# First loads of a decoder layer: x and the first weights in smaller pieces, ahead of the other loads

## The chip, the core and the metric

The program runs on one core of a Trainium2 chip. The metric is the device time of one execution in microseconds (us), lower is better; the median of three executions before the change is 1202.25 us. TensorE (PE) multiplies matrices, VectorE (DVE) and ScalarE (ACT) do elementwise work, GpSimd (POOL) does little here, and SyncE (SP) issues nearly all transfers between HBM and the on-chip memory SBUF. PSUM is the memory that TensorE accumulates in.

## The reference

One layer of a decoder with 16 learned tokens put ahead of 256 input tokens (with 112 inert slots of padding in front, which the kernel leaves out: it works on T = 272 columns). Cut to what matters:

```
u    = rmsnorm(h, attn_norm) * vmask          # h: tokens x 2048
proj = u @ w_in                               # 2048 x 6144
aq, ak, av, rq, rk, rv, rg = split(proj)
ya = rmsnorm(diff_attention(aq, ak, av, lam, slopes, valid), attn_subln) * (1 - lam_init)
yr = rmsnorm(retention(rq, rk, rv, log_g), ret_norm) * silu(rg)
h  = h + concat(ya, yr) @ w_out
u  = rmsnorm(h, ffn_norm) * vmask
h  = h + (silu(conv(u @ w_gate)) * (u @ w_up)) @ w_down
out = rmsnorm(h, final_norm)[:, padding + 16:]
```

Everything is float32. `diff_attention` adds a distance term to the scores (ALiBi), which the kernel reads from a prepared array, `alibi`.

## The kernel before

All products are made in three passes of a rounded format: each operand is split into a high part and a remainder, and hi*hi, hi*lo and lo*hi are summed in PSUM. For a weight chunk (1024 KB, 128 partitions x 2048 columns, tile `raw`) ACT casts a half of 1024 columns into `whi`, and DVE subtracts to give `wlo`; for x, ACT scales a k-tile of 128 features (`xhi`) and DVE makes `xlo`. `raw`, `whi` and `wlo` have three buffers each, so the cast of a half waits until PE is through with the half three before it.

There are 48 chunks of input projection, 16 of `w_out`, 88 of gate and up, 44 of `w_down`. The norm of x is not applied ahead of the first product: the outputs are multiplied by `rstd1` afterwards, and `rstd1` comes from the squares of x, summed by ACT and DVE into `acc`, summed over partitions by a matmul with `ones` (tile `psx`, L204), and put through a chain of twelve DVE operations (from `ms`, L206, to `rstd`, L127).

The change lies in the start, a loop over four blocks `c` of four k-tiles each. Since x arrives together with the weights here, the first four output tiles (`mm_93` to `mm_96`) are accumulated side by side: for each k-tile 12 matmuls (4 tiles x 3 passes, L189 to L191). `w_first[c]` is a 1024 KB chunk that holds the four tiles' weights of block `c`. After the start, `gemm` computes one output tile per chunk (L261 to L263), 48 matmuls each: the fifth tile from the first chunk of `w_in`, and so on; `prep` (L99, L100) splits their weights. In the text, "chunk 4" is the first of `w_in`, "chunk 7" the fourth.

SP issues the transfers in the order in which they stand. A load into `raw` waits until the buffer's former content has been split. The constants `lq`, `c_ident`, `c_alibi`, `c_attn_subln`, `c_ret_norm`, `c_ffn_norm` and `c_conv_w` are loaded on the same queue. `c_alibi` has 86 partitions; all other loads of the start have 128. ACT needs it for `bias` (L302), DVE needs `c_attn_subln` for a small scaling (L233).

A scheduler merges the program's parts into one instruction order for each engine; each engine then runs in that order and waits on semaphores. `klz`, a small tile of the attention, and later `htok`, which holds the residual by tokens, share one room of the pool `big` (tag `htok`).

Of the kernel before, what the change touches and what calls it, by code (L numbers as in the profile page):

```python
# [10 lines left out]
F32 = mybir.dt.float32  # L11
# [3 lines left out]
AF = mybir.ActivationFunctionType  # L15
ALU = mybir.AluOpType
# [3 lines left out]
P = 128  # L20
D = 2048
# [3 lines left out]
T = META + SEQ  # L25
# [28 lines left out]
def trunk_kernel(ctx, tc, a, out):  # L54
    nc = tc.nc
    V, S, PE = nc.vector, nc.scalar, nc.tensor

    cp = ctx.enter_context(tc.tile_pool(name="const", bufs=1))
    big = ctx.enter_context(tc.tile_pool(name="big", bufs=1))
    wp = ctx.enter_context(tc.tile_pool(name="wts", bufs=1))  # L60
# [19 lines left out]
    raw = {}  # L80
# [24 lines left out]
    def ahead(hf):  # L105
        while state["dma"] < len(chunks) and state["dma"] <= (hf + 4) // 2:
            load(state["dma"])
            state["dma"] += 1
        while state["prep"] < 2 * len(chunks) and state["prep"] <= hf + 2:
            prep(state["prep"])  # L110
            state["prep"] += 1

    def rsqrt(x, shape, pool, tag, o=None, tags=None):
        tags = tags or (tag + "i", tag + "t", tag + "o")
        i = pool.tile(shape, I32, tag=tags[0], name=tag + "i")
        V.tensor_scalar(out=i, in0=x.bitcast(I32), scalar1=1, scalar2=None,
                        op0=ALU.logical_shift_right)
        V.tensor_scalar(out=i, in0=i, scalar1=-1, scalar2=0x5F3759DF,
                        op0=ALU.mult, op1=ALU.add)
        y = i.bitcast(F32)  # L120
        t = pool.tile(shape, F32, tag=tags[1], name=tag + "t")
        if o is None:
            o = pool.tile(shape, F32, tag=tags[2], name=tag + "o")
        for it in range(3):
            V.scalar_tensor_tensor(out=t, in0=y, scalar=-0.5, in1=x, op0=ALU.mult, op1=ALU.mult)
            V.tensor_tensor(out=t, in0=t, in1=y, op=ALU.mult)
            V.scalar_tensor_tensor(out=o, in0=t, scalar=1.5, in1=y, op0=ALU.add, op1=ALU.mult)  # L127
            y = o
        return o
# [26 lines left out]
    FN = [(Q0, NQ), (0, T), (0, T), (Q0, NQ)]  # L156
    with tc.tile_pool(name="start", bufs=2) as st:
        acc = st.tile([P, 4, T], F32, name="acc", bufs=1)
        for c in range(4):
            xr = st.tile([P, 4, T + 1], F32, tag="xr", bufs=4, name=f"xr{c}")  # L160
            rw = wp.tile([P, D], F32, tag="raw", bufs=3, name=f"raw{c}")
            cuts = [(0, 1), (1, 2), (2, 4)] if c == 0 else [(0, 2), (2, 4)] if c == 1 else [(0, 4)]
            for b, e in cuts:
                nc.sync.dma_start(out=xr[:, b:e], in_=a["x"][:, 4 * c + b:4 * c + e])
                nc.sync.dma_start(out=rw[:, b * 512:e * 512], in_=a["w_first"][c][:, b * 512:e * 512])  # L165
            for half in range(2):
                whi = wp.tile([P, 1024], F32R, tag="whi", bufs=3, name=f"whi{2 * c + half}")
                wlo = wp.tile([P, 1024], F32R, tag="wlo", bufs=3, name=f"wlo{2 * c + half}")
                for jj in range(2):
                    j = 2 * half + jj  # L170
                    k = 4 * c + j
                    xg = xr[:, j, T:T + 1]
                    S.activation(out=xhi[:, k], in_=xr[:, j, :T], func=AF.Copy, scale=xg)
                    V.scalar_tensor_tensor(out=xlo[:, k], in0=xr[:, j, :T], scalar=xg,
                                           in1=xhi[:, k].bitcast(F32),
                                           op0=ALU.mult, op1=ALU.subtract)
                    if c == 0 or jj == 0:
                        n = 512 if c == 0 else 1024
                        d = slice(jj * 512, jj * 512 + n)
                        src = rw[:, j * 512:j * 512 + n]  # L180
                        S.copy(out=whi[:, d], in_=src)
                        V.tensor_tensor(out=wlo[:, d], in0=src, in1=whi[:, d].bitcast(F32),
                                        op=ALU.subtract)
                    for t, (t0, n) in enumerate(FN):
                        b = jj * 512 + t * P
                        wh, wl = whi[:, b:b + P], wlo[:, b:b + P]
                        xh, xl = xhi[:, k, t0:t0 + n], xlo[:, k, t0:t0 + n]
                        o = first[t][:, :n]
                        PE.matmul(o, wh, xh, start=(k == 0), stop=False)  # L189
                        PE.matmul(o, wh, xl, start=False, stop=False)  # L190
                        PE.matmul(o, wl, xh, start=False, stop=(k == KT - 1))  # L191
            if c == 0:
                S.activation(out=acc, in_=xr[:, :, :T], func=AF.Square)
            else:
                sq = st.tile([P, 4, T], F32, tag="sq", name=f"sq{c}")
                S.activation(out=sq, in_=xr[:, :, :T], func=AF.Square)
                V.tensor_tensor(out=acc, in0=acc, in1=sq, op=ALU.add)
        state["dma"], state["prep"] = 4, 8
        ahead(8)
        with tc.high_priority():  # L200
            V.tensor_tensor(out=acc[:, 0:2], in0=acc[:, 0:2], in1=acc[:, 2:4], op=ALU.add)
            V.tensor_tensor(out=acc[:, 0], in0=acc[:, 0], in1=acc[:, 1], op=ALU.add)
            pst = psx[:, 0]
            PE.matmul(pst[:, :T], ones, acc[:, 0], start=True, stop=True)  # L204
            ms = st.tile([P, T], F32, name="ms", bufs=1)
            V.tensor_scalar(out=ms, in0=pst[:, :T], scalar1=EPS, scalar2=None, op0=ALU.add)  # L206
            rsqrt(ms, [P, T], st, "r1", rstd1)
# [60 lines left out]
    with ExitStack() as p1:  # L268
# [211 lines left out]
        for h in range(AH):  # L480
            q = ap_.tile([P, NQ], F32, tag="q", name=f"q{h}")
            k = ap_.tile([P, T], F32, tag="k", name=f"k{h}")
# [12 lines left out]
            for m in range(2):  # L495
# [3 lines left out]
                                op=ALU.subtract)  # L499
# [3 lines left out]
                                op=ALU.subtract)  # L503
            side.extend(att_tasks(h, q2, (k2, kl), v))
        for kind, r in RSEQ:
# [9 lines left out]
            k = ap_.tile([P, T], F32, tag="k", name=f"rk{r}")  # L515
# [18 lines left out]
        htok = big.tile([P, 2, D], F32, tag="htok", name="htok")  # L534
        acc2 = yp.tile([P, NQ], F32, name="acc2")
        for j in range(KT):
            xr = ap_.tile([P, NQ], F32, tag="g0", name=f"xres{j}")
# [6 lines left out]
            else:  # L544
                sq = ap_.tile([P, NQ], F32, tag="rt", bufs=4, name=f"hsq{j}")
# [4 lines left out]
                                   in1=ghi[:, j].bitcast(F32), op0=ALU.mult, op1=ALU.subtract)  # L550
# [16 lines left out]
    with ExitStack() as p2:  # L567
# [4 lines left out]
        for f in range(NF):  # L572
# [3 lines left out]
            c = fw.tile([P, SEQ], F32, tag="c", name=f"fc{f}")  # L576
            V.tensor_scalar(out=c, in0=g[:, 0:SEQ], scalar1=cw[:, f, 0:1], scalar2=None,
                            op0=ALU.mult)
            for i in (1, 2):
                V.scalar_tensor_tensor(out=c, in0=g[:, i:i + SEQ], scalar=cw[:, f, i:i + 1],  # L580
                                       in1=c, op0=ALU.mult, op1=ALU.add)
# [8 lines left out]
                            op=ALU.subtract)  # L590
# [138 lines left out]
def build(arrs):  # L729
    import concourse.bacc as _bacc  # L730
    import concourse.tile as _tile
    from concourse import mybir as _mybir

    nc = _bacc.Bacc("TRN2", target_bir_lowering=False, num_devices=1)
    arrays, args = {}, {}
    for name, v in arrs.items():
        arrays[f"in_{name}_dram"] = v
        args[name] = nc.dram_tensor(f"in_{name}_dram", v.shape, _mybir.dt.from_np(v.dtype),
                                    kind="ExternalInput").ap()
    o = nc.dram_tensor("out_0_dram", (SEQ, D), _mybir.dt.from_np(np.dtype("float32")),  # L740
                       kind="ExternalOutput").ap()
    with _tile.TileContext(nc, schedule_with_timeline_sim=True) as tc:
        trunk_kernel(tc, args, o)
    return nc, arrays
# [8 lines left out]
```

## Time and profile before

| | us |
|---|---|
| median of 3 runs (1201.59 to 1203.49) | 1202.25 |
| the profiled execution | 1201.67 |
| its span, first to last instruction | 1199.9 |
| PE busy in it | 1183.2 |
| DVE busy | 790.1 |
| ACT busy | 557.5 |

The span is what the rows below divide up; 1.77 us of the profiled execution lie outside of it. All stretches are given in us from the span's start. In the timeline the starts of successive matmuls show their pace better than their lengths, since they overlap.

### The profile page before, as it was taken

How to read it: one execution, taken by the hardware profiler on the slowest of the kernel's cores; microseconds unless marked ns; L12 is line 12 of the kernel's file. 1: busy time of each engine (PE TensorE's matmuls, PEld its weight loads, DVE VectorE, ACT ScalarE, POOL GpSimd, SP SyncE). 2: the span in 40 equal slices, each digit the busy share in tenths (PEclk: the TensorE clock that was granted, in tenths of full speed). 3: DMA queues.
4: the chain of work that ended last, by engine and by line, in shares of the span. 5: the costliest groups of instructions: out<-in, count | busy, mean ns of one | idle time of the engine just before them, and what ended most of it. 6: DMA issues, size and time to landing. Idle time of an engine off the chain costs nothing.

```text
span 1199.9 us, 21288 instructions
## 1 busy us (share of the span) xinstructions
PE 1183.2 (99%) x8811; PEld 1132.3 (94%) x8811; DVE 790.1 (66%) x1423; ACT 557.5 (46%) x865; POOL 2.0 (0%) x7
## 2 busy tenths in 40 slices
PE   8999999999999999999999999999999999999996
PEld 7999999999999999999999999999999988888885
DVE  6888887668766667666666666666666545454544
ACT  6476665554445544444444444444444434343442
POOL 0000000000000000000000000000000000000000
PEclk9999999999999999999999999999999999999999
DMA  8443434444446554555555554555555655555452
GB/s 298 154 169 141 161 131 178 145 156 172 141 159 232 198 187 176 176 188 192 183 176 181 195 188 176 179 196 186 177 181 190 227 177 196 189 179 203 179 189 92
DMA packets 34817, 215.71 MB, mean 180 GB/s; under 512 B 4194, under 2 KB 7882, under 8 KB 9760
## 3 DMA queue, kind: packets, MB, share of 16 engines
q1 hardware_dynamic: 34288, 212.58, 50.2%
q8 instruction: 69, 1.13, 0.4%
q0 software_dynamic: 144, 1.05, 0.2%
q10 hardware_dynamic: 288, 0.72, 0.2%
q14 instruction: 28, 0.23, 0.1%
HBM read 212.24 MB, written 2.10 MB: 179 GB/s over the span
## 4 chain that ended last, share of the span: by engine, by line
PE 95%; DMA 2%; DVE 2%; SPq 0%; ACT 0%; issue 0%; DVEq 0%; ACTq 0%
PE mm L261 24%; PE mm L262 24%; PE mm L263 23%; PE o L612 7%; PE o L614 7%; PE o L613 7%; DMA raw<-in_w_first_dram 1%; PE po L365 1%; DMA xr<-in_x_dram 1%; PE sc L315 0%; PE sc L313 0%; DVE wlo L100 0%; PE pa L353 0%; PE rs L405 0%; SPq L165 0%
## 5 line engine op out<-in xcount | busy, mean ns | idle before, releaser
L99 ACT CAST whi<-raw 128x1024 fp32r<-128x1024 f32 x381 | 399.7, 1049 | 553.4 <-PE mm L262 296.7
L100 DVE TENSOR_TENSOR wlo<-raw,whi 128x1024 fp32r<-128x1024 f32 x381 | 466.2, 1224 | 275.7 <-ACT whi L99 272.4
L261 PE MATMUL mm<-ghi,whi 128*128 128x258 f32 (+1 forms) x1408 | 396.9, 282 | 0.0
L263 PE MATMUL mm<-ghi,wlo 128*128 128x258 f32 (+1 forms) x1408 | 396.7, 282 | 0.0
L262 PE MATMUL mm<-glo,whi 128*128 128x258 f32 (+1 forms) x1408 | 396.1, 281 | 0.0
L262 PEld LDWEIGHTS mm<-glo,whi 128*128 128x128 f32 x1408 | 266.4, 189 | 0.0
L261 PEld LDWEIGHTS mm<-ghi,whi 128*128 128x128 f32 x1408 | 266.0, 189 | 0.0
L263 PEld LDWEIGHTS mm<-ghi,wlo 128*128 128x128 f32 x1408 | 265.8, 189 | 0.0
L261 PE MATMUL mm<-xhi,whi 128*128 128x272 f32 (+1 forms) x688 | 200.4, 291 | 0.0
L262 PE MATMUL mm<-xlo,whi 128*128 128x272 f32 (+1 forms) x688 | 198.8, 289 | 0.0
L263 PE MATMUL mm<-xhi,wlo 128*128 128x272 f32 (+1 forms) x688 | 197.8, 288 | 0.5 <-DVE wlo L100 0.5
L613 PE MATMUL o<-wlo,fhi 128*128 128x512 f32 x340 | 134.2, 395 | 0.0
L614 PE MATMUL o<-whi,flo 128*128 128x512 f32 x340 | 134.1, 395 | 0.0
L263 PEld LDWEIGHTS mm<-xhi,wlo 128*128 128x128 f32 x688 | 129.5, 188 | 0.8 <-DVE wlo L100 0.8
L261 PEld LDWEIGHTS mm<-xhi,whi 128*128 128x128 f32 x688 | 129.7, 188 | 0.1
L262 PEld LDWEIGHTS mm<-xlo,whi 128*128 128x128 f32 x688 | 129.6, 188 | 0.1
L612 PE MATMUL o<-whi,fhi 128*128 128x512 f32 x340 | 120.8, 395 | 0.0
L614 PEld LDWEIGHTS o<-whi,flo 128*128 128x128 f32 x340 | 64.1, 188 | 15.0
L613 PEld LDWEIGHTS o<-wlo,fhi 128*128 128x128 f32 x340 | 64.1, 188 | 14.9
L612 PEld LDWEIGHTS o<-whi,fhi 128*128 128x128 f32 x340 | 64.0, 188 | 14.9
L261 PE MATMUL mm<-yhi,whi 128*128 128x258 f32 x256 | 73.2, 288 | 0.4 <-ACT whi L99 0.4
L262 PE MATMUL mm<-ylo,whi 128*128 128x258 f32 x256 | 72.3, 283 | 0.0
(227 smaller groups left out, 1070.0 us busy)
## 6 DMA issues: line engine op xcount, KB each, us to landing
raw<-in_w_in_dram SPq DMA_DIRECT2D x44, 1024.0 KB, 4.9
raw<-in_w_gate_dram SPq DMA_DIRECT2D x44, 1024.0 KB, 4.9
raw<-in_w_up_dram SPq DMA_DIRECT2D x44, 1024.0 KB, 4.8
raw<-in_w_down_dram SPq DMA_DIRECT2D x44, 1024.0 KB, 4.8
raw<-in_w_out_dram SPq DMA_DIRECT2D x16, 1024.0 KB, 4.8
xres<-in_x_dram SPq DMA_DIRECT2D x16, 129.0 KB, 3.8
raw<-in_w_first_dram SPq DMA_DIRECT2D x2, 1024.0 KB, 13.3
raw<-in_w_first_dram SPq DMA_DIRECT2D x3, 512.0 KB, 7.4
```

The costliest lines, as they stand in the source:

```text
L99: S.copy(out=hi, in_=src)
L100: V.tensor_tensor(out=lo, in0=src, in1=hi.bitcast(F32), op=ALU.subtract)
L261: PE.matmul(ps[:, :n], wh, xh, start=(k == 0), stop=False)
L262: PE.matmul(ps[:, :n], wh, xl, start=False, stop=False)
L263: PE.matmul(ps[:, :n], wl, xh, start=False, stop=(k == KT - 1))
L365: PE.matmul(ps[:QT, i * P:(i + 1) * P], at[j][:n, i - j], vt[:n, j], start=(j == 0), stop=(j == i))
L612: PE.matmul(po[m], ah, wh, start=(k == 0), stop=False)
L613: PE.matmul(po[m], ah, wl, start=False, stop=False)
L614: PE.matmul(po[m], al, wh, start=False, stop=(k == NF - 1))
```

## The change

The transfers of all four blocks are issued ahead of the arithmetic loop, so that they stand in front of all other loads. The first block comes in four pieces of one k-tile, the others in two pieces of two k-tiles. The first piece of x is issued from ACT's queue, and the first piece of weights is cut into two of 256 columns, which ACT and DVE split one by one. The fourth chunk `raw3` gets no buffer of the three in `raw`: it lies in the room of `klz` and `htok`, so it doesn't wait for a buffer. The squares of x stand behind all four blocks in the code.

```
+        xrs, rws = [], []
         for c in range(4):
             xr = st.tile([P, 4, T + 1], F32, tag="xr", bufs=4, name=f"xr{c}")
-            rw = wp.tile([P, D], F32, tag="raw", bufs=3, name=f"raw{c}")
-            cuts = [(0, 1), (1, 2), (2, 4)] if c == 0 else [(0, 2), (2, 4)] if c == 1 else [(0, 4)]
+            if c < 3:
+                rw = wp.tile([P, D], F32, tag="raw", bufs=3, name=f"raw{c}")
+            else:
+                rw = big.tile([P, D], F32, tag="htok", name="raw3")
+            cuts = [(b, b + 1) for b in range(4)] if c == 0 else [(0, 2), (2, 4)]
             for b, e in cuts:
-                nc.sync.dma_start(out=xr[:, b:e], in_=a["x"][:, 4 * c + b:4 * c + e])
-                nc.sync.dma_start(out=rw[:, b * 512:e * 512], in_=a["w_first"][c][:, b * 512:e * 512])
+                lead = c == 0 and b == 0
+                (nc.scalar if lead else nc.sync).dma_start(
+                    out=xr[:, b:e], in_=a["x"][:, 4 * c + b:4 * c + e])
+                step = 256 if lead else (e - b) * 512
+                for d in range(b * 512, e * 512, step):
+                    nc.sync.dma_start(out=rw[:, d:d + step], in_=a["w_first"][c][:, d:d + step])
+            xrs.append(xr)
+            rws.append(rw)
+        for c in range(4):
+            xr, rw = xrs[c], rws[c]
...
                     if c == 0 or jj == 0:
                         n = 512 if c == 0 else 1024
-                        d = slice(jj * 512, jj * 512 + n)
-                        src = rw[:, j * 512:j * 512 + n]
-                        S.copy(out=whi[:, d], in_=src)
-                        V.tensor_tensor(out=wlo[:, d], in0=src, in1=whi[:, d].bitcast(F32),
-                                        op=ALU.subtract)
+                        step = 256 if k == 0 else n
+                        for b in range(0, n, step):
...
+        for c in range(4):
             if c == 0:
-                S.activation(out=acc, in_=xr[:, :, :T], func=AF.Square)
+                S.activation(out=acc, in_=xrs[c][:, :, :T], func=AF.Square)
```

**SP's queue.** Before, from the third block on (`raw_252` is its weights, `raw_323` those of the fourth block, `raw_393` is chunk 4):

```order
L165 DMA raw_252<-in_w_first_dram 128x2048
L164 DMA xr_322<-in_x_dram 128x1092
L215 DMA lq<-in_lambda_qk_dram 128x256
L211 DMA c_ident<-in_ident_dram 128x128
L211 DMA c_alibi<-in_alibi_dram 86x816
L211 DMA c_attn_subln<-in_attn_subln_dram 128x1
L211 DMA c_ret_norm<-in_ret_norm_dram 128x2
L165 DMA raw_323<-in_w_first_dram 128x2048
L211 DMA c_ffn_norm<-in_ffn_norm_dram 128x16
L211 DMA c_conv_w<-in_conv_w_dram 128x132
L87 DMA raw_393<-in_w_in_dram 128x2048
```

And now, from the last half of the fourth block (`raw_125`; `raw_402` is chunk 4, `raw_404` chunk 5):

```order
L169 DMA xr_124<-in_x_dram 128x546
L173 DMA raw_125<-in_w_first_dram 128x1024
L87 DMA raw_402<-in_w_in_dram 128x2048
L230 DMA lq<-in_lambda_qk_dram 128x256
L226 DMA c_ident<-in_ident_dram 128x128
L226 DMA c_alibi<-in_alibi_dram 86x816
L226 DMA c_attn_subln<-in_attn_subln_dram 128x1
L226 DMA c_ret_norm<-in_ret_norm_dram 128x2
L226 DMA c_ffn_norm<-in_ffn_norm_dram 128x16
L226 DMA c_conv_w<-in_conv_w_dram 128x132
L87 DMA raw_404<-in_w_in_dram 128x2048
```

The fourth block and chunk 4 have moved ahead of the constants; the chunk behind them is now chunk 5.

**ACT, end of the start.** Before (`whi_326`, `whi_358`: fourth block; `whi_399`, `whi_403`: chunk 4):

```order
L196 ACTIVATE sq_390<-xr_322 128x1088
L302 ACTIVATE bias_479<-c_alibi 86x816
L230 ACTIVATE lam<-lam 128x2
L181 CAST whi_326<-raw_323 128x1024
L181 CAST whi_358<-raw_323 128x1024
L99 CAST whi_399<-raw_393 128x1024
L99 CAST whi_403<-raw_393 128x1024
```

Now (`whi_328`, `whi_360`: fourth block; `whi_408`, `whi_412`: chunk 4; `whi_416`: chunk 5):

```order
L195 CAST whi_328<-raw_125 128x1024
L185 ACTIVATE xhi_68<-xr_124 128x272 x2
L211 ACTIVATE sq_399<-xr_124 128x1088
L195 CAST whi_360<-raw_125 128x1024
L99 CAST whi_408<-raw_402 128x1024
L317 ACTIVATE bias_488<-c_alibi 86x816
L99 CAST whi_412<-raw_402 128x1024
L245 ACTIVATE lam<-lam 128x2
L99 CAST whi_416<-raw_404 128x1024
```

The operation that needs `c_alibi` has moved behind the fourth block's casts, between the two casts of chunk 4.

**DVE, from chunk 5 to chunk 7.** Before, the first half of chunk 7 (`wlo_701`) stands behind the attention's operands of two heads:

```order
L501 CAST k_0_464<-k_458 64x272 x2
L100 TENSOR_TENSOR wlo_640<-raw_397,whi_639 128x1024
L498 TENSOR_TENSOR q_0_463<-q_457,q_0_463 64x258 x2
...
L344 COPY vt_475<-pv_603 100x128
L345 COPY vt_475<-pv_603 86x256
L100 TENSOR_TENSOR wlo_701<-raw_585,whi_700 128x1024
L100 TENSOR_TENSOR wlo_736<-raw_585,whi_735 128x1024
```

Now the first half of chunk 7 is `wlo_710`, the second `wlo_745`:

```order
L516 CAST k_0_473<-k_467 64x272 x2
L100 TENSOR_TENSOR wlo_710<-raw_594,whi_709 128x1024
L513 TENSOR_TENSOR q_0_472<-q_466,q_0_472 64x258
...
L359 COPY vt_484<-pv_612 100x128
L360 COPY vt_484<-pv_612 86x256
L100 TENSOR_TENSOR wlo_745<-raw_594,whi_744 128x1024
```

The first half of chunk 7 has moved ahead of those operands, and only the second half stands behind them. Further up, `wlo_417` (first half of chunk 5) now stands ahead of `ms`, where `wlo_404` (second half of chunk 4) stood; the matmul on `psx` has moved on PE from inside the fourth block to the thirteenth matmul of the fifth tile that stands behind that block.

## Rows read from the trace of the kernel before

**Rows 1.** The page: busy us, share of the span, instructions.

```profile
PE 1183.2 (99%) x8811; PEld 1132.3 (94%) x8811; DVE 790.1 (66%) x1423; ACT 557.5 (46%) x865; POOL 2.0 (0%) x7
```

**Rows 2.** PE's waits in the whole span: us in total, times, longest.

```profile
PE mm L189 <- ACT whi L181: 3.7, 2, 3.2
...
PE mm L191 <- DVE wlo L182: 0.7, 1, 0.7
PE mm L263 <- DVE wlo L100: 0.5, 1, 0.5
```

**Rows 3.** Timeline of PE: start, us, instruction, [idle before, releaser].

```profile
17.61 0.66 PE L191 MATMUL mm<-xhi,wlo 128*128 128x258 f32 x4
...
22.05 0.28 PE L189 MATMUL mm<-xhi,whi 128*128 128x258 f32 x1
...
23.52 0.28 PE L189 MATMUL mm<-xhi,whi 128*128 128x258 f32 x1
...
29.77 0.39 PE L189 MATMUL mm<-xhi,whi 128*128 128x258 f32 x1 [3.16 <-ACT whi L181]
...
36.96 0.62 PE L204 MATMUL psx<-acc,ones 128*128 128x272 f32 x2
...
37.54 0.29 PE L190 MATMUL mm<-xlo,whi 128*128 128x272 f32 x1
...
38.16 0.29 PE L263 MATMUL mm<-xhi,wlo 128*128 128x272 f32 x1
...
56.21 0.29 PE L262 MATMUL mm<-xlo,whi 128*128 128x272 f32 x1
57.03 0.39 PE L263 MATMUL mm<-xhi,wlo 128*128 128x272 f32 x1 [0.54 <-DVE wlo L100]
```

**Rows 4.** Stretches: busy time of each engine, granted clock, DMA share, GB/s.

```profile
5.00:10.60 5.60, 5.41 (x24) 5.26 (x24) 2.88 (x7) 3.77 (x8) 0.00 (x0) 1.00 0.92 301
11.00:15.00 4.00, 4.00 (x34) 4.00 (x34) 3.68 (x8) 3.98 (x8) 0.00 (x0) 1.00 1.03 424
15.00:18.00 3.00, 3.00 (x27) 3.00 (x26) 3.00 (x5) 3.00 (x6) 0.00 (x0) 1.00 1.01 406
...
30.80:34.10 3.30, 3.30 (x16) 3.08 (x16) 3.30 (x5) 1.05 (x1) 0.00 (x0) 0.50 0.17 50
```

**Rows 5.** Timeline of ACT: the second block's last cast, then the waits.

```profile
14.74 1.04 ACT L181 CAST whi<-raw 128x1024 fp32r<-128x1024 f32 x1
...
26.04 0.89 ACT L302 ACTIVATE bias<-c_alibi 86x816 f32<-86x816 f32 x1 [3.04 <-DMA c_alibi<-in_alibi_dram]
...
28.67 2.00 ACT L181 CAST whi<-raw 128x1024 fp32r<-128x1024 f32 x2 [1.66 <-DMA raw<-in_w_first_dram]
```

**Rows 6.** Timeline of SP's queue: start and us of an issue.

```profile
10.04 0.33 SPq L211 DMA_DIRECT2D c_ident<-in_ident_dram  x1
15.28 0.33 SPq L165 DMA_DIRECT2D raw<-in_w_first_dram  x1
```

**Rows 7.** Transfers: KB of one, median us from issue to landing.

```profile
c_alibi<-in_alibi_dram SPq DMA_DIRECT2D x1, 274.1 KB
...
c_ident<-in_ident_dram SPq DMA_DIRECT2D x1, 64.0 KB, 9.5
```

**Rows 8.** Timeline of DVE.

```profile
14.17 0.91 DVE L174 SCALAR_TENSOR_TENSOR xlo<-xr,xhi 128x272 fp32r<-128x272 f32 x2
15.00 1.28 DVE L197 TENSOR_TENSOR acc<-acc,sq 128x1088 f32<-128x1088 f32 x1
16.20 1.22 DVE L182 TENSOR_TENSOR wlo<-raw,whi 128x1024 fp32r<-128x1024 f32 x1
...
37.62 0.44 DVE L206 TENSOR_SCALAR ms<-psx 128x272 f32<-128x272 f32 x1 [0.73 <-PE psx L204]
...
55.75 2.36 DVE L100 TENSOR_TENSOR wlo<-raw,whi 128x1024 fp32r<-128x1024 f32 x2
```

More of the change, by code (lines that the diff above doesn't have):

```diff
@@ L178, in trunk_kernel @@
                         n = 512 if c == 0 else 1024
-                        d = slice(jj * 512, jj * 512 + n)
-                        src = rw[:, j * 512:j * 512 + n]
-                        S.copy(out=whi[:, d], in_=src)
-                        V.tensor_tensor(out=wlo[:, d], in0=src, in1=whi[:, d].bitcast(F32),
-                                        op=ALU.subtract)
+                        step = 256 if k == 0 else n
+                        for b in range(0, n, step):
+                            d = slice(jj * 512 + b, jj * 512 + b + step)
+                            src = rw[:, j * 512 + b:j * 512 + b + step]
+                            S.copy(out=whi[:, d], in_=src)
+                            V.tensor_tensor(out=wlo[:, d], in0=src, in1=whi[:, d].bitcast(F32),
+                                            op=ALU.subtract)
                     for t, (t0, n) in enumerate(FN):
@@ L191, in trunk_kernel @@
                         PE.matmul(o, wl, xh, start=False, stop=(k == KT - 1))
+        for c in range(4):
             if c == 0:
-                S.activation(out=acc, in_=xr[:, :, :T], func=AF.Square)
+                S.activation(out=acc, in_=xrs[c][:, :, :T], func=AF.Square)
             else:
                 sq = st.tile([P, 4, T], F32, tag="sq", name=f"sq{c}")
-                S.activation(out=sq, in_=xr[:, :, :T], func=AF.Square)
+                S.activation(out=sq, in_=xrs[c][:, :, :T], func=AF.Square)
                 V.tensor_tensor(out=acc, in0=acc, in1=sq, op=ALU.add)
```

## The prediction

> **What bounds the kernel now.** The page comes first: TensorE is busy for 1183.2 of 1199.9 us [rows 1], so a change can win only where it waits or runs slowly. The list of its waits names three that matter: 3.2 us in one piece for a cast of `w_first` weights, 0.7 for a remainder `wlo`, 0.5 for another [rows 2]. The timeline and the stretches place them. The longest ends at 29.77, in front of the fourth block [rows 3]: ACT's cast there waited for the transfer until 28.67 [rows 5]. [...]
>
> Why was the fourth block's chunk late? It was issued at 15.28 [rows 6], behind `c_alibi`, which landed at 26.04; the chunk landed 2.6 us after it [rows 5]. `c_ident`, issued just ahead of `c_alibi`, landed at 10.04 + 9.5 = 19.5 [rows 6, 7]. So 6.5 us passed from the one landing to the next, for 274.1 KB [rows 7]: 43 GB/s, while full stretches move 406 to 424 GB/s [rows 4]. `c_alibi` is a slow transfer, and what is queued behind it waits for a part of it.
>
> [...]
>
> **The start, to 17.6.** I cost the smaller pieces of the first block at nothing, in either direction. What PE does up to 17.61 (four remainders of the second block's second half) is tied to DVE: `xlo` of the block from 14.17, the sum into `acc` from 15.00, `wlo` from 16.20 to 17.42 [rows 8], and PE uses it at 17.61 [rows 3]. On ACT the cast for it follows its neighbours without a gap [rows 5]. The order of these operations is the same after the change, and the bytes of blocks one and two are as many. So an earlier first matmul, or an earlier rise of the clock, ends as a wait in front of this `wlo`. Work that covers it: DVE's chain; without it the gain would be the half microsecond before the first matmul.
>
> **From there to the fifth tile.** Before, PE goes from 17.61 to 38.16, the first matmul with chunk 4's remainder [rows 3], in 20.55 us. Between them lie 114 matmuls of blocks two to four and of the fifth tile, 114 x 0.1225 = 14.0 us, and the `psx` matmul, which moves 0.45 us of time (from 36.96 to the L190 at 37.54, less one matmul of 0.125) [rows 3] behind this point. Can everything now be ready in 14.0 us? Per half-chunk PE needs 24 x 0.1225 = 2.94 us. DVE needs 0.91 for two `xlo`, 1.22 for `wlo`, and half of a sum of 1.28: 2.77 [rows 8]. ACT's cast is 1.04 [rows 5], and its other work is lighter than DVE's. In the new order the operations alternate half by half, so DVE keeps ahead. The fourth block lands about 21.6 (next part) and its second half is wanted at 17.6 + 88 x 0.1225 = 28.4. So the point of 38.16 comes at **31.6**, 6.55 us earlier; `psx` gives 0.45 back, which leaves **6.1**.
>
> **`c_alibi` afterwards.** In front of `c_ident` stand two chunks of 1024 KB more, the fourth block's and chunk 4. 2 x 1.049 MB at 415 GB/s (between 406 and 424 [rows 4]) are 5.05 us, so `c_ident` lands at 24.6 and `c_alibi` at 26.04 + 5.05 = **31.1** (30.9 to 31.5 by the slower and faster rates). Chunk 4 is ahead of it and safe; the fourth block, with one chunk less in front, lands 3 us before `c_ident`. Chunk 5 now stands where the late chunk stood, and lands 2.6 us after `c_alibi`, at 33.7.
>
> Behind ACT's `bias` (0.89 [rows 5]) waits the cast of chunk 4's second half: 31.1 + 0.9 + 1.04 = 33.05, and its `wlo` at 34.3; PE wants the latter at 31.6 + 25 x 0.125 + 0.45 = 35.2. DVE's scaling by `c_attn_subln` lands as late and holds the last sum of `acc` until about 32.0; PE wants it for `psx` at 33.1. Both pass with 0.9 us to spare.
>
> What is late next is the chain of the norm. The cast of chunk 5 ends at 33.7 + 1.05 = 34.75, its `wlo`, which now stands ahead of `ms`, at 36.0, so `ms` starts at 36.0 although `psx` is done by 33.7. Before, DVE went from `ms` at 37.62 to the end of the two `wlo` of chunk 7 at 58.11 [rows 8], 20.5 us; the same list has one `wlo` less now (1.22) and 0.3 us of waits that fall away: 19.0. It ends at 55.0 with the second half of chunk 7. PE reaches that half so: before, it wanted chunk 7's first remainder at 56.21 + 0.125 = 56.33 and got it at 57.03, 0.7 late [rows 3]. From 38.16 to 56.33 are 18.17 us; with `psx` PE is there at 31.6 + 18.17 + 0.45 = 50.2, finds it ready (its place is earlier now), and needs the second half 24 matmuls of 0.125 later, at 53.2. Pause: 55.0 - 53.2 = **1.8 us** in place of 0.7.
>
> **Sum.** 6.1 + 0.7 - 1.8 = **5.0 us**. The rest of the program keeps its order behind the first heads, and PE bounds it. Against the profiled execution's 1201.67 us that gives 1196.6. The median of the runs, 1202.25, is 0.6 above this execution, so I forecast **1197.2 us**.
>
> **Bounds.** Every microsecond by which `c_alibi` lands sooner or later moves the last pause by as much. At 29.3 or sooner there is none: gain 6.8. `klz` is now cleared only after the fourth block is split, on POOL, which has nothing else to do, long before its use; nothing for that. Whether a pause of 1.8 us lowers the clock the trace doesn't show: the 0.7 us one did not (the twelve matmuls from 22.05, right behind it, take 1.47 us [rows 3]), the 3.2 us one did. [...]
>
> **Rivals.**
> [...]
> *No pause at all:* `c_alibi` sooner, or a shorter chain: 1195.4. The margin of 1.8 us is larger than the spread of the transfer rates, which speaks against it.
> *The smaller pieces move slower.* From 5 to 10.6, with the first block's pieces, the stretch has 301 GB/s [rows 4]. If blocks three and four (3.2 MB) moved so, they would take 10.7 instead of 7.8 us, `c_alibi` would land 2.9 us later, and 2.1 us of gain would be left, 1200.1, about no change. Against it: the second block was already cut in two, and the stretch from 11 to 15, where its casts fall, has 424, no less than the 406 after it with whole chunks. [...]
> *Slower than before:* `c_alibi` lands so late that ACT holds chunk 4's second half and PE stands there for over 3 us. [...]
> *The change does nothing:* not possible for the pause before the fourth block, unless the first queue entries wait for landings longer than shown.
>
> **Chances.** Forecast within 1 us of 5.0: 0.5; the clock falls: 0.15; no pause: 0.2; slow pieces: 0.11; slower: 0.04. A measurement of this kernel tells about 0.2% (2.4 us) from no change, so faster is 0.87, the same 0.10, slower 0.03. Eight in ten lie from 1195.0 to 1199.4: the lower end is the gain of 6.8 with 0.4 us for the spread of runs, the upper the fallen clock with `c_alibi` another microsecond late.
>
> **What would show it.** Right: no wait of PE for a cast of `w_first` weights over 0.5 us behind 17.6; no stretch at half clock between 26 and 34; the first matmul with chunk 4's remainder near 31.6; ACT's `bias` idle before it until about 31.1, put down to `c_alibi`; one wait of PE for DVE's `wlo` between 52 and 56, in the second half of chunk 7. Wrong: `bias` starting by 29 or after 33; PE waiting for chunk 4's or 5's cast; a wait in blocks two to four, which would mean that DVE's 2.77 us against 2.94 is too tight.

## The result and the profile after

The changed kernel takes 1196.01 us (median of 4, 1195.63 to 1196.83) where the kernel before took 1202.32 beside it: ratio 0.9948, 95% interval 0.9935 to 0.996. That is 6.3 us faster; 5.0 had been forecast. The profiled execution took 1195.63 us with a span of 1193.9 us.

The page, engines' busy time, to be read against [rows 1]:

```profile
PE 1180.8 (99%) x8811; PEld 1130.6 (95%) x8811; DVE 789.3 (66%) x1424; ACT 557.1 (47%) x866; POOL 2.0 (0%) x7
```

PE's waits (the first is that of the warm-up at the start, as before):

```profile
PE psx L150 <- DVE warm L138: 1.5, 1, 1.5
PE mm L203 <- ACT xhi L185: 0.5, 1, 0.5
PE mm L278 <- DVE wlo L100: 0.4, 1, 0.4
PE mm L276 <- ACT whi L99: 0.4, 1, 0.4
```

The wait of 3.2 us for a cast of `w_first` [rows 2] has gone. The 0.5 is the first matmul of all. The last, for `whi`, was 0.4 us in the kernel before as well. The one for `wlo` is the forecast pause at chunk 7; the timeline of PE has it at the end:

```profile
17.25 0.66 PE L205 MATMUL mm<-xhi,wlo 128*128 128x258 f32 x4
...
31.24 0.29 PE L278 MATMUL mm<-xhi,wlo 128*128 128x272 f32 x1
...
32.75 0.62 PE L219 MATMUL psx<-acc,ones 128*128 128x272 f32 x2
...
53.02 0.29 PE L277 MATMUL mm<-xlo,whi 128*128 128x272 f32 x1
53.76 0.39 PE L278 MATMUL mm<-xhi,wlo 128*128 128x272 f32 x1 [0.45 <-DVE wlo L100]
```

From the second block's remainders to the first remainder of chunk 4 PE needs 31.24 - 17.25 = 13.99 us where it needed 20.55 [rows 3]. The stretches (PE, PEld, DVE, ACT, POOL; then granted clock, DMA share, GB/s) are those of [rows 4] and two more:

```profile
5.00:10.60 5.60, 5.44 (x26) 5.44 (x27) 3.85 (x9) 4.43 (x9) 0.00 (x0) 1.00 0.98 300
11.00:15.00 4.00, 4.00 (x35) 4.00 (x34) 3.71 (x7) 4.00 (x7) 0.00 (x0) 1.00 1.04 416
15.00:18.00 3.00, 3.00 (x27) 3.00 (x26) 3.00 (x5) 3.00 (x7) 0.00 (x0) 1.00 1.03 416
18.00:22.00 4.00, 4.00 (x35) 4.00 (x34) 4.00 (x5) 4.00 (x6) 0.00 (x0) 1.00 1.05 415
24.00:26.00 2.00, 2.00 (x19) 2.00 (x18) 2.00 (x4) 1.32 (x2) 0.00 (x0) 1.00 0.20 73
30.80:34.10 3.30, 3.30 (x27) 3.22 (x27) 1.60 (x3) 2.38 (x4) 0.00 (x0) 1.00 0.54 216
```

The stretch at half clock is gone: 27 matmuls from 30.80 to 34.10 in place of 16. From 24 to 26 the DMA share is only 0.20, at 73 GB/s: what moves there are rows of `c_alibi` and the small constants, and little else was left in the queue. SP issued no load between `c_conv_w` and chunk 5, and the profile puts its wait down to chunk 4's landing (`raw<-in_w_in_dram`):

```profile
21.48 0.33 SPq L226 DMA_DIRECT2D c_conv_w<-in_conv_w_dram  x1
25.15 0.80 SPq L87 DMA_DIRECT2D raw<-in_w_in_dram  x2
```

```profile
SPq L87 <- DMA raw<-in_w_in_dram: 3.3, 1, 3.3
```

So a low share is not by itself the mark of `c_alibi`. In the kernel before, the share was 1.02 on the way to its landing at 26.04, only at a lower rate (289 GB/s), and the trough of [rows 4] came after it had landed:

```profile
20.00:26.00 6.00, 5.25 (x43) 5.04 (x42) 3.57 (x6) 3.00 (x6) 0.00 (x0) 1.00 1.02 289
```

ACT's timeline of the changed kernel shows who waits for `c_alibi` now:

```profile
25.18 1.05 ACT L99 CAST whi<-raw 128x1024 fp32r<-128x1024 f32 x1 [0.68 <-PE mm L204]
30.22 0.88 ACT L317 ACTIVATE bias<-c_alibi 86x816 f32<-86x816 f32 x1 [3.99 <-DMA c_alibi<-in_alibi_dram]
31.01 1.03 ACT L99 CAST whi<-raw 128x1024 fp32r<-128x1024 f32 x1
33.06 1.05 ACT L99 CAST whi<-raw 128x1024 fp32r<-128x1024 f32 x1 [0.92 <-DMA raw<-in_w_in_dram]
```

ACT is idle for 4 us before `bias`, more than the 3.04 of before [rows 5], and it costs nothing there, because chunk 4 has landed and its first half is cast. On DVE the delay arrives by `c_attn_subln` and by chunk 5, whose remainder (34.14) stands ahead of `ms` (chunk 5 was also issued late, at 25.15):

```profile
30.41 0.15 DVE L248 TENSOR_SCALAR sub<-c_attn_subln 128x1 f32<-128x1 f32 x1 [1.16 <-DMA c_attn_subln<-in_attn_subln_dram]
32.07 1.23 DVE L100 TENSOR_TENSOR wlo<-raw,whi 128x1024 fp32r<-128x1024 f32 x1 [0.97 <-ACT whi L99]
34.14 1.23 DVE L100 TENSOR_TENSOR wlo<-raw,whi 128x1024 fp32r<-128x1024 f32 x1 [0.77 <-ACT whi L99]
35.28 0.43 DVE L221 TENSOR_SCALAR ms<-psx 128x272 f32<-128x272 f32 x1
...
52.48 1.22 DVE L100 TENSOR_TENSOR wlo<-raw,whi 128x1024 fp32r<-128x1024 f32 x1
```

The remainder at 52.48 ends at 53.70, and PE goes on at 53.76.

### The profile page after: what moved, and what is told of

It reads as the page before. It is cut to its first block, busy times and chain, and to the rows that moved or that the text cites. A ratio compares the mean times of both kernels' runs of the same rounds, so it can differ in the third digit from the quotient of the medians.

```text
span 1193.9 us, 21303 instructions
## 1 busy us (share of the span) xinstructions
PE 1180.8 (99%) x8811; PEld 1130.6 (95%) x8811; DVE 789.3 (66%) x1424; ACT 557.1 (47%) x866; POOL 2.0 (0%) x7
## 4 chain that ended last, share of the span: by engine, by line
PE 98%; DVE 1%; ACT 0%; DMA 0%; issue 0%; DVEq 0%; ACTq 0%
PE mm L276 24%; PE mm L277 24%; PE mm L278 24%; PE o L627 7%; PE o L629 7%; PE o L628 7%; PE po L380 1%; PE mm L203 1%; PE mm L204 1%; PE mm L205 1%; PE sc L330 0%; PE sc L328 0%; PE pa L368 0%; PE rs L420 0%; DMA raw<-in_w_first_dram 0%; PE ph L570 0%
```

## The experiments

The theory: the pause of before came from `c_alibi`, whose transfer is slow because of its 86 partitions, together with the place of the fourth block behind it; the change puts the fourth block and chunk 4 ahead of it, and what is left of its delay is the pause at chunk 7. Rivals: the fourth block was late for want of a buffer; the smaller first pieces carry part of the gain; any new order would do.

**e1: the kernel before, `alibi` at 128 partitions.**

```
-    base = const("alibi", [QT, 3, T])
+    base = const("alibi", [P, 3, T])[:QT]
...
```

(The lines left out pad the prepared array by rows of zeros; so they do in e2 and e8.)

> The kernel before, with the array alibi padded by rows of zeros from 86 to 128 partitions (they are loaded and never read; all else as before, order and buffers too). Theory: the pause in front of the fourth block comes from c_alibi, which moves its 274 KB at a tenth of the rate of other loads and delays the chunk queued behind it. Then the padded c_alibi (418 KB) lands about 1 us after c_ident, near 20.5 us in place of 26.0; the fourth block's chunk lands near 23 in place of 28.7; PE has no wait for a cast of w_first weights over 0.5 us behind 17.6 us and no stretch at half clock from 30 to 34; the time falls by 4.5 us (3.2 of pause and 1.3 of low clock) to 6 us. Rival: the chunk is late because it is issued late (15.28 us, when a buffer of the ring comes free); then the pause stays over 2 us and the time falls by less than 1.5 us.

1196.27 us against 1201.91, ratio 0.9953 (0.9941 to 0.9964): 5.6 us of gain without any change of order. ACT:

```profile
22.27 0.88 ACT L302 ACTIVATE bias<-c_alibi 86x816 f32<-86x816 f32 x1
...
24.61 2.00 ACT L181 CAST whi<-raw 128x1024 fp32r<-128x1024 f32 x2 [1.23 <-DMA raw<-in_w_first_dram]
```

`bias` doesn't wait any more, and the fourth block's cast starts at 24.61 in place of 28.67 [rows 5], though its transfer was issued at 14.70, hardly earlier than the 15.28 of [rows 6]. So the late issue isn't what delayed it; the slow transfer ahead was. PE's longest wait for a cast of `w_first` is 0.9 us, at 10.1, and the clock from 30.80 to 34.10 is 1.00. The chunk came 1.6 us later than I expected of it.

**e2: the changed kernel, `alibi` at 128 partitions** (the same edit).

> The changed kernel with the same padding of alibi to 128 partitions (nothing else). Theory: c_alibi lands about 1 us after c_ident, near 25 us in place of about 30, so ms starts when psx is done (about 33.5 in place of 35.3), DVE ends its list before PE wants the second half of chunk 7, and the wait of 0.65 us there goes: 0.4 to 0.8 us faster than the changed kernel, 6.7 to 7.1 us faster than before. Rival: the wait at chunk 7 is set by DVE's own list, whenever ms starts: no difference to the changed kernel (within 0.3 us).

1195.25 us; the changed kernel's medians are 1196.01, 1195.87 and 1195.72 in three series, so 0.5 to 0.8 less. `ms` starts at 33.93 in place of 35.28 and PE has no wait at chunk 7. `bias` starts at 26.79, 0.22 us after ACT came free and put down to `c_alibi`: later than the 25 expected. Padding takes away the pause, but the last bytes still trickle in; from 25 to 26 us the transfers have a share of 0.18 at 52 GB/s. The packet records of the trace have there the last rows of `c_alibi` (until 26.29) and the small constants; SP issued no other load from 21.92 to 25.34.

**e7: the changed kernel, `c_alibi` in two transfers, without padding.**

```
-    base = const("alibi", [QT, 3, T])
+    base = cp.tile([QT, 3, T], F32, name="c_alibi")
+    for p0, p1 in ((0, 64), (64, QT)):
+        nc.sync.dma_start(out=base[p0:p1], in_=a["alibi"][p0:p1])
```

> The changed kernel with c_alibi loaded by two transfers, of 64 and of 22 partitions, without padding (one more entry in SP's queue; else the same order up to chunk 5). Theory: the slowness comes from the number 86 of partitions, not from the place, the size or the tile; two transfers of other numbers move at the rate of the other loads or near it. The later one lands within 1.5 us of c_ident, near 25 us, and the wait at chunk 7 goes: 0.4 to 0.8 us faster than the changed kernel, as with the padding. Rival: anything under 128 partitions is slow, or the number of rows decides: c_alibi lands at 29 or later and the time is that of the changed kernel.

1194.96 us (1194.64 to 1195.0) beside 1195.87 of the changed kernel: 0.9 less, a little more than expected. `bias` starts at 26.96 right behind a cast, without a wait (later than the 25 expected), and PE has no wait at chunk 7. The same bytes in the same place of the queue land about 3 us sooner, cut into 64 and 22 partitions. Bytes, place and tile are the same: it is the cut by partitions.

The packet records of the traces show it directly. `c_alibi` moves in rows of 3264 bytes, one for each partition. In the changed kernel its 86 rows run from 23.33 to 29.35 us, which is 6.0 us at 0.143 us a row: two rows at a time on average (86 x 0.143 / 6.0 = 2.0). In e7 they run from 23.06 to 26.37, 3.3 us at 0.169 a row: 4.4 at a time.

**e8: the changed kernel, `alibi` at 89 partitions.**

```
-    base = const("alibi", [QT, 3, T])
+    base = const("alibi", [89, 3, T])[:QT]
...
```

> The changed kernel with alibi padded from 86 to 89 partitions by rows of zeros that are never read (283.7 KB in place of 274.1). [...] Then ACT's bias holds the cast of chunk 4's second half until about 39, PE stands there for 5 to 6 us, and the time is 5 to 8 us above the changed kernel, that is 1 us faster to 2 us slower than before: this is the rival 'slower' of the prediction, made on purpose. [...]

1202.01 us beside 1202.38 of the kernel before, ratio 1.0 (0.9991 to 1.0009): three partitions more take the whole gain away. ACT and PE, of the same execution:

```profile
36.73 0.88 ACT L317 ACTIVATE bias<-c_alibi 86x816 f32<-86x816 f32 x1 [10.33 <-DMA c_alibi<-in_alibi_dram]
```

```profile
37.67 1.26 PE L219 MATMUL psx<-acc,ones 128*128 128x272 f32 x2 [4.59 <-DVE acc L217]
```

`c_alibi` lands at 36.73 in place of 30.22, 6.5 us later for 3.5% more bytes. In the packet records its 89 rows run from 23.15 to 36.18, 13.0 us at 0.150 us a row: one row at a time (1.0 on average), where the 86 rows went two at a time in 6.0 us. The 39 us of the expectation stand on a landing near 37, that is on half the rate of 86 partitions, which was an estimate of mine: no run had shown it before. This one does, 13.0 us in place of 6.0; why 86 rows go two at a time and 89 one at a time is not shown. One point of the expectation was wrong: PE waits not for ACT's cast but for `psx`, because DVE's last sum of `acc` stands behind `sub`, which waits for `c_attn_subln` in the queue behind `c_alibi` (7.63 us on DVE). The stretches show what the clock does after 4.59 us:

```profile
36.00:38.00 2.00, 0.33 (x1) 0.33 (x2) 0.69 (x3) 1.27 (x2) 0.00 (x0) 0.93 0.07 25
38.00:40.00 2.00, 2.00 (x8) 1.77 (x8) 1.29 (x2) 1.12 (x3) 0.00 (x0) 0.50 0.10 37
40.00:42.00 2.00, 2.00 (x14) 2.00 (x13) 1.38 (x2) 1.52 (x2) 0.00 (x0) 0.72 0.58 127
```

**e3: the new order with the pieces of before.** In the program's order chunk 4 then stands behind `c_alibi`.

```
-            cuts = [(b, b + 1) for b in range(4)] if c == 0 else [(0, 2), (2, 4)]
+            cuts = [(0, 1), (1, 2), (2, 4)] if c == 0 else [(0, 2), (2, 4)] if c == 1 else [(0, 4)]
...
-                lead = c == 0 and b == 0
+                lead = False
...
-                        step = 256 if k == 0 else n
+                        step = n
```

> The changed kernel's order (all four blocks' loads ahead of the loop, the fourth chunk in the residual's room, squares behind) with the pieces of before: first block in three, second in two, third and fourth whole, nothing on ACT's queue, no piece of 256 columns. In the program's order chunk 4 stands behind c_alibi here. Theory: pieces give nothing, the place relative to c_alibi gives all. The fourth block then lands ahead of c_alibi, near 21 us, and PE doesn't wait for it; but chunk 4 lands about 2.6 us after c_alibi, near 31, where PE wants its first cast at about 28.5: a wait for chunk 4's cast of 2.5 to 3.5 us in front of the fifth tile, with or without a fall of the clock behind it. Time 2 to 3.5 us faster than before, so 3 to 4.5 us slower than the changed kernel. Rival: the smaller pieces of the first block carry part of the gain by starting PE earlier: then the second block's remainders come later than 17.25 us by 0.3 or more and that much is lost besides. Rival 2: any order that puts the fourth block ahead gives the full gain: 6 us faster than before.

1196.69 us, ratio 0.9957 (0.9945 to 0.9969): 5.2 us faster than before, 0.7 to 1.0 slower than the changed kernel. Chunk 4 landed at 32.04 (expected: near 31), but it cost less than expected. PE:

```profile
31.08 0.75 PE L205 MATMUL mm<-xhi,wlo 128*128 128x258 f32 x4 [0.73 <-DVE wlo L196]
...
33.14 0.38 PE L276 MATMUL mm<-xhi,whi 128*128 128x272 f32 x1
33.37 0.28 PE L277 MATMUL mm<-xlo,whi 128*128 128x272 f32 x1
34.40 0.39 PE L278 MATMUL mm<-xhi,wlo 128*128 128x272 f32 x1 [0.75 <-DVE wlo L100]
```

There isn't one wait of 3 us but several of under 1 (one more, of 0.55, stands at 21.26 in the third block, where the kernel before waits 0.75 and the changed kernel, with its halves, not at all). The first is DVE again: `sub` waited there until 29.73 for `c_attn_subln`, and the fourth block's remainder stood behind it. The first remainder of chunk 4 comes 3.16 us after that of the changed kernel (31.24), and 0.6 of it comes back, since nothing is late at chunk 7 then. The single profile, at 1197.70 the longest of its five executions, overstates the loss. So the size was over-estimated, and rival 2 (any order gives all) is near, but not level. The first block's old pieces help e3, by 0.8 to 0.9 us if they are worth here what they are in e9 below: e9, which has them too but keeps chunk 4 ahead and the halves, gains 7.4 us, and e3 5.2.

**e5: the changed kernel, the fourth chunk in the ring of three buffers.**

```
-            if c < 3:
-                rw = wp.tile([P, D], F32, tag="raw", bufs=3, name=f"raw{c}")
-            else:
-                rw = big.tile([P, D], F32, tag="htok", name="raw3")
+            rw = wp.tile([P, D], F32, tag="raw", bufs=3, name=f"raw{c}")
```

> The changed kernel with one edit: the fourth chunk takes a buffer of the ring of three again, not the residual's room. Its issue then waits until a buffer has been split (15.28 us before), all loads behind it on SP's queue wait as well, and in the program's order chunk 4 stands behind c_alibi. Theory: the room matters because it lets chunk 4 go ahead of c_alibi. Without it the fourth block still lands ahead of c_alibi and PE doesn't wait for it, c_alibi lands near 28.5, chunk 4 near 31, and PE waits 2.5 to 3.5 us for chunk 4's cast in front of the fifth tile; 2 to 3.5 us faster than before, 3 to 4.5 slower than the changed kernel. Rival: the room is of no consequence, the order of the loads alone gives the gain: within 0.6 us of the changed kernel.

1197.31 us, ratio 0.996 (0.9948 to 0.9972): 4.6 faster than before, 1.3 to 1.6 slower than the changed kernel: that is what the room for the fourth chunk is worth. The profile, at 1197.92 the longest of the five executions, shows more, and a part of it lies in the start (second block's remainders at 18.04). Chunk 4's cast starts at 31.66, and its first remainder waits until 34.02. As in e3 the waits are short (0.34 and 0.74 us on PE), and the forecast loss of 3 to 4.5 us was too large.

**a0 and a0b: the changed kernel again; e9 and e9b: with the first block's pieces of before** (the last two edits of e3, and `[(0, 1), (1, 2), (2, 4)]` for the first block alone).

> The changed kernel once more, as the measure for the other three. Theory: 5.5 to 6.5 us faster than before; c_alibi lands near 30, one wait of PE for a remainder of chunk 7 of 0.4 to 0.9 us. What a second profile shows of the start (second block's remainders at 17.25 us in the first one, 17.61 before) tells whether 0.36 us is a gain or the spread of executions: a value from 17.2 to 17.3 again speaks for a gain, one of 17.6 or later for spread.

> The changed kernel with the first block's pieces as before: three pieces, none on ACT's queue, none of 256 columns; blocks three and four still in halves, the fourth in the residual's room, chunk 4 ahead of the constants. Theory: the first block's pieces give nothing, because the second block's remainders hang on DVE's chain and the transfers: within 0.4 us of the changed kernel, first matmul at 5.1 to 5.2 us, second block's remainders between 17.2 and 17.7. Rival: they carry 0.3 to 0.5 us or more of the gain: slower than the changed kernel by that, remainders at 17.6 or later in each profile.

> The changed kernel, a third time, as the measure for the other two: 1195.8 to 1196.1 us by its medians so far.

> The changed kernel with the first block's pieces as before, once more. It came out 0.84 us below the changed kernel (1195.03 against 1195.87), with the second block's remainders at 17.40 us, inside the spread of the start seen so far (17.25 to 17.60 with the changed start). Theory: the first block's pieces are worth nothing, the difference is spread: within 0.5 us of the changed kernel now. Rival: the smaller pieces cost time: again 0.6 to 1.0 us below it.

Medians: 1195.87 and 1195.72 for the changed kernel, 1195.03 and 1194.79 with the old pieces. Both times the new pieces are slower, by 0.84 and 0.93 us; the expectation of "nothing" fails, though single executions of the second pair overlap (1194.45 to 1195.89 against 1195.33 to 1195.83). Where does the time go? One execution of each, in us:

| | first matmul | second block's remainders | `bias` | wait at chunk 7 | SP's last issue | span | span's end after it |
|---|---|---|---|---|---|---|---|
| changed | 5.16 | 17.25 | 30.22 | 0.4 | 1189.18 | 1193.9 | 4.7 |
| a0 | 5.12 | 17.60 | 30.97 | 0.6 | 1189.80 | 1194.5 | 4.7 |
| a0b | 5.11 | 17.76 | 29.57 | none | 1189.05 | 1193.7 | 4.7 |
| e9 | 5.63 | 17.40 | 30.33 | 0.4 | 1189.29 | 1193.3 | 4.0 |
| e9b | 5.09 | 17.08 | 30.25 | 0.6 | 1189.14 | 1193.1 | 4.0 |
| before | 5.19 | 17.61 | 26.04 | 0.5 | 1195.67 | 1199.9 | 4.2 |

Not in the start: the remainders of the second block come at 17.25 to 17.76 with the new pieces and at 17.08 to 17.40 with the old (over all profiles 17.25 to 18.04 and 17.08 to 17.61), although PE waits 2.1 us (e9) for casts there in place of 0.5. The 0.36 us that the first profile seemed to gain is spread. The difference is at the very end: at SP's last transfer of the output the kernels agree within their spread, and then the span goes on for 4.7 us in place of 4.0.

The landing records of the traces place it further. The last transfer lands 3.0 us after that issue in all 14 profiles. What differs stands behind it, where only the program's closing waits and drains are left: 1.65 us in the changed kernel, 0.95 in e9 and e9b, 1.20 in the kernel before.

**e11: the changed kernel, the first piece of x on SP's queue.**

```
-                (nc.scalar if lead else nc.sync).dma_start(
+                nc.sync.dma_start(
```

> The changed kernel with one edit: the first piece of x is issued by SP, at the head of its queue, and not by ACT; all pieces and their sizes stay. In six profiles with the piece on ACT's queue the span ends 4.6 to 4.7 us after SP's last output transfer is issued, in six without it 4.0 to 4.3 us. Theory: the issue on ACT costs about 0.5 us at the end of the program, whatever it gives at the start: the span ends 4.0 to 4.3 us after the last issue, and the time is 0.4 to 0.9 us below the changed kernel (1195.7 to 1196.0), near 1195.0. Rival: the smaller pieces of the first block cost it (their receipts or their count): the end stays at 4.6 or more and the time is within 0.3 us of the changed kernel.

1195.80 us, and the span ends 1194.8 - 1190.21 = 4.6 us after the last issue. The theory falls: it isn't ACT's queue. The end of 4.6 to 4.7 us goes with the first block's finer cut (the six kernels that have it 4.6 to 4.7, the five without it 4.0 to 4.3; behind the last landing 1.57 to 1.65 and 0.95 to 1.29). Why a finer cut at the start makes the closing longer no row shows; that stays open. This run also tests the start: the first matmul comes at 4.71, 0.4 us sooner, and the second block's remainders at 17.54 all the same.

**e10: both edits that lay below the changed kernel, e7's and e9's.**

> The two edits that came out below the changed kernel together: c_alibi in two transfers of 64 and 22 partitions, and the first block's pieces as before. Theory (the pieces are worth nothing): like the two transfers alone, 0.9 us below the changed kernel, 7.2 to 7.4 below the kernel before. Rival (the pieces cost 0.8 us by themselves): the two gains add, 1.5 to 1.8 us below the changed kernel.

1194.68 us (1194.43 to 1194.87) against 1202.05, ratio 0.9942 (0.9929 to 0.9954): the fastest version by its median, 7.4 us faster than before and 1.0 faster than the changed kernel. The gains don't add (0.1 below e9b, 1.0 below a0b, in one series): the rival's 1.5 to 1.8 fails, and beside the kernel before it gains as much as e7 alone (7.4 in both). Its last issue is the earliest of all, at 1188.52, and its span ends 4.3 us later.

## Why the prediction was right, and what was off

*The pause and the half clock before the fifth tile.* Right, in place, cause and size: 13.99 us where 14.0 were worked out, with 0.1225 us a matmul by the twelve from 22.05 to 23.52 [rows 3]. The range counts 1.3 us for a fallen clock; at that pace the 16 matmuls of the half clock, 3.30 us [rows 4], would have taken 1.96, so 1.34 more was lost there. e1 takes the cause away in the old order and gets 5.6 us, e8 makes it worse in the new order and loses everything.

*The start, costed at nothing.* Right for the start, within its spread: an earlier first matmul (e11), more waits (e9) and an earlier full pace (below) all end in front of the same remainders. The reason given was too narrow: the waits fall not in front of the last `wlo` but of ACT's casts (0.79 us at 13.34 in a0b, 1.17 at 10.39 in e9), and DVE waits for ACT there as well (0.83 us at 10.83 in the changed kernel's profile, 0.90 at 12.85 in e7), so ACT and the transfers hold the start, not DVE's chain alone. Wrong for the program: the finer first block costs 0.8 to 0.9 us, and 0.7 of that shows as a later end of the span. Where `c_alibi` comes in two transfers nothing clear of the noise is left of it (e7 and e10 both gain 7.4 us over the kernel before beside them). No row of before could tell that.

*`c_alibi` at 31.1.* It landed at 30.22, and between 29.57 and 31.38 in six executions with the new order of loads; the bounds given (30.9 to 31.5) were too narrow, since they took the spread of the transfer rates alone (which gives 31.0 to 31.2). Chunk 5 at 33.06 (33.7) and `ms` at 35.28 (36.0) follow from it.

*The pause at chunk 7, 1.8 us.* This is the term that was mis-sized: PE waited 0.6 us by the matmuls' pace (53.76 - 53.02, less one of 0.125), because `c_alibi` was 0.9 us sooner (`ms` 0.7) and DVE's list took 18.4 us (35.28 to 53.70), not 19.0. The chain itself is right: where `c_alibi` lands at 29.57 there is no pause, at 30.97 one of 0.6, in e11 at 31.38 one of 1.1; where it lands before 27 (e2, e7) there is none. The limit of 29.3 that I gave lies a few tenths too low.

*The sum.* By SP's last issue the program gained 1195.67 - 1189.18 = 6.49 us: 6.92 at chunk 4's remainder (38.16 - 31.24, with 0.36 of spread in it), less 0.45 for `psx`, the pause at chunk 7 about as long as before. Less 0.5 at the end that makes 6.0, the difference of the spans. The forecast was 6.1 + 0.7 - 1.8. Two terms stood in no sum, 0.36 of spread at the start and 0.5 lost at the end; that they nearly cancel is luck.

*The rivals.* The clock didn't fall at the new pause: waits of 0.45 to 1.11 us there, one of 1.17 at 13.61 in e5 and one of 1.56 at 10.07 in e9b leave the pace at 0.12 us a matmul; those of 3.16 and 4.59 us are followed by 0.50. "No pause" was nearest to what happened, and is what a0b shows. Slower pieces: halves, transfers of 512 KB that follow one another, move at 415 and 416 GB/s in the changed kernel, the whole chunks of before at 406 [rows 4]. "Slower", by a late `c_alibi`, is e8; a landing at 36.73 is even with before. I let ACT's cast decide it; DVE's `acc` does.

## What to carry to other kernels

Here a load that was slow for its shape delayed what was queued behind it: with 128 partitions in place of 86 ahead of it, the fourth block's cast started at 24.61 in place of 28.67. The DMA share did not show it (1.02 from 20 to 26 us before); the time from one landing to the next did, 6.5 us for 274 KB. Look for that before moving other loads around it: padding 86 partitions to 128 in the kernel before was worth 5.6 us, nearly as much as the whole reordering (cutting them into 64 and 22 was tried in the changed kernel alone). What stood between two loads in the queue mattered more here than their issue times (in e1 the fourth block's was 14.70, before 15.28), and a small operation that waited for a constant (`sub`, 0.15 us) held DVE's whole list, in e8 for 7.63 us. Finer first pieces bought nothing here, where the work behind them was held by other engines, and their cost showed only at the end of the program.

## What was not expected of the hardware

- 86 partitions (274.1 KB) and 89 (283.7 KB) differ by 6.5 us in landing. In e8 the issue behind `c_alibi` took SP 5.21 us (at 18.25), where the same issue took 0.35 in the changed kernel: with the slower transfer ahead the issue was long too. What held it is not shown.
- In the first 10.6 us of the changed kernel's profile the clock column reads 1.00, yet 26 matmuls take 5.44 us, 0.21 each, the pace of the stretch at 0.50 [rows 4]. The trace's clock records begin only at 10.03 us there, at 7.34 in a0 and at 5.12 in e9, and the full pace of 0.12 us begins with them (in e9 from the first matmul on). So the 1.00 ahead of that stands for no record, not for a clock that was granted. The start of the full pace differs between executions of one program and made no difference behind 17 us.
